# New numbers in a list scheduler's model, a fixed order for the first weight loads, and 15 matmuls of the identity while TensorE waits for them

## The chip, the cores and the metric

The kernel runs on one core of one Trainium2 chip. The metric is the device time of one execution in microseconds (us), the median of several runs. The core has a tensor engine (PE in the profile, its weight loads PEld), a vector engine (DVE), a scalar engine (ACT), GpSimd (POOL), and a queue on SyncE (SP) that issues the DMA transfers.

## The reference, cut to what is computed

A block of a diffusion transformer, two layers deep, over 256 latent and 256 context tokens of width 1024, all in float32. For each layer:

```python
mod = silu(c) @ w_ada[l] + b_ada[l]             # shift, scale and gate, for both sublayers
h = x * (1 + sc1) + sh1
q, k, v of 4 mixers, gates = split(h @ w_in[l])
y_i = latent attention, 2-D neighbourhood attention, differential attention, grouped-query attention
acc = sum_i sigmoid(gates_i) * (y_i @ w_branch[l, i])
x = layer_norm(ALPHA * x + g1 * (acc @ w_out[l]))
h = x * (1 + sc2) + sh2
x = layer_norm(ALPHA * x + g2 * ((silu(h @ Wg) * (h @ Wu)) @ w_down[l]))
```

The context tokens go through the same first layer; in the second only their keys and values are needed. The output is the latent stream.

## The kernel before

**Precision.** Every large product is made of three matmuls: an operand is split into a rounded high part and the rest (`hh`, `hl` for activations, `wh`, `wl` for weights, `fh`, `fl` for the rows of `w_out`), and `mm3` adds high by high, high by low and low by high in PSUM. For each weight tile of 128x1024 that SP loads into a `wr` buffer, ACT casts the high part (`wh` or `fh`) and DVE subtracts (`wl` or `fl`); then the `wr` buffer can take the next load. PE works mostly on moving tiles of 512 or 256 columns.

**Who decides the order.** No instruction is placed by hand. The body of the kernel only records operations in a `Plan`; `forward` then makes a list schedule of all of them. For every operation it has a modelled duration (`price`), for DMA transfers a model of one shared queue, and among the operations that are ready on an engine it takes the one with the best priority. The priorities come from `backward`, which schedules the same operations from the end. Ten passes alternate, and the one with the shortest modelled length is emitted. So a number in `price` has no direct effect on the chip: it changes which operation stands ahead of which on PE, ACT, DVE and SP. On the chip every engine goes through its list in that order, and an operation that waits holds up everything behind it on its engine. All recorded instructions have L540, the line that emits them; the strips, below, are written out at L538.

**The start.** `first_h` makes the first layer's shift and scale in eight chunks q, while weights stream in. For a chunk SP loads two tiles of `w_ada0`; the function `strips` multiplies each with the conditioning vector `cc` in float32 (four matmuls of 32x256 beside one another, into `st`; the profile counts them as eight). ACT copies `st` to `y`, PE transposes it with the identity `ident` (two transposes), DVE adds up `ada` and makes `G`, ACT makes the modulated `raw` from `x`, `ada` and `G`, and DVE casts `hh` and subtracts `hl`. `early(q)` loads the part of the input weights `w_a0` that this chunk needs and splits it; the matmuls `o<-hh,wh`, `mm<-hh,wh` and so on then use chunk q's `hh` and `hl`.

**The rest of a layer.** The input projection, the four mixers with their heads, the branch projections and `w_out`, then the feed-forward part. The shift and scale vectors of later places are made by DVE in passes over 128x1024 tiles of `w_ada` (`y<-wr,silbc` and `raw<-wr,silbc`), spread among the other work.

Of the kernel before, what the change touches and what calls it, by code (L numbers as in the profile page):

```python
# [11 lines left out]
F32R = mybir.dt.float32r  # L12
# [192 lines left out]
class Op:  # L205
    __slots__ = ("eng", "meth", "args", "kw", "phase", "idx", "preds", "succs", "npred", "tiles", "cost",
                 "prio", "prio2", "rest", "nafter", "start", "end", "est", "nrot", "bytes", "dge", "ins", "lab")

# [23 lines left out]
class Plan:  # L232
# [16 lines left out]
    def record(self, eng, meth, args, kw):  # L249
# [5 lines left out]
        if pos:  # L255
            if "out" in kw:
                ins += pos
            else:
                outs.append(pos[0])
                ins += pos[1:]  # L260
        op.preds, op.succs, op.tiles = set(), [], []
        for w, views in ((False, ins), (True, outs)):
# [15 lines left out]
        return op  # L278

    def price(self, op, ins, outs):  # L280

        eng, kw = op.eng, op.kw
        if eng == "tensor":
            if op.meth == "matmuls":
                return sum(k["rhs"].free() for k in kw["each"]) / 2400 / 4 * (1 if kw["each"][0]["rhs"].dtype == F32R else 4) + 0.1
            if op.meth == "transpose":
                n = kw["in_"].shape[0]
                return max(64, n) * 2.1 / 2400
            n = max(64, kw["rhs"].free())
            return n / 2400 + 0.0026 if kw["rhs"].dtype == F32R else n * 4 / 2400 + 0.43  # L290
        n = max([v.free() for v in outs + ins] or [1])
# [12 lines left out]
        if eng == "gpsimd":  # L304
            if kw.get("op") == ALU.pow:
                return 0.3 + n * 0.17
            return 0.16 + n * 2.2e-3
        op_bytes = 1
        for v in (outs or ins):
            op_bytes = v.shape[0] * v.free() * 4  # L310
        op.bytes = op_bytes
        op.dge = 0.65 if outs and ins else 0.46
        return 0.05
# [21 lines left out]
    def backward(self, order):  # L335
# [4 lines left out]
        for op in order:  # L340
            after = set(op.succs)
            for t in op.tiles:
                if t.next is not None:
                    after |= t.next.users
            op.nafter, op.rest = len(after), 0.0
            heirs[op] = after
# [9 lines left out]
        while done < len(order):  # L356
# [10 lines left out]
            if e == "sync":  # L367
                dma = max(dma, t + 0.95) + max(op.bytes / 360e3, op.dge)
                free[e] = dma - 0.95
                op.prio2 = dma + 1.1  # L370
            else:
                free[e] = op.prio2 = t + op.cost
            done += 1
            for p in before[op]:
                p.rest = max(p.rest, op.prio2 + SEE[p.eng].get(e, SEE_OTHER[p.eng]))
                p.nafter -= 1
                if p.nafter == 0:
                    ready[p.eng].append(p)
# [5 lines left out]
    def forward(self):  # L384
        ops = self.ops
        for op in ops:
            op.npred = len(op.preds)
            op.est = 0.0
            op.nrot = 0
            for t in op.tiles:  # L390
                t.left, t.slot, t.waiters, t.next, t.users = 0, None, [], None, set()
# [70 lines left out]
        while done < len(ops):  # L462
# [16 lines left out]
            if e == "sync":  # L479
                dge_free = max(op.end, dge_free) + op.dge  # L480
                dma_free = max(dge_free + 0.65, dma_free) + op.bytes / 360e3
                op.end = dma_free + 0.95
                free[e] = max(free[e], dma_free - 2.5)
# [4 lines left out]
            for s in op.succs:  # L488
                s.est = max(s.est, op.end + SEE[e].get(s.eng, SEE_OTHER[e]))
                s.npred -= 1  # L490
                if s.npred == 0 and s.nrot == 0:
                    push(s)
# [50 lines left out]
class Net:  # L543
# [157 lines left out]
    def first_h(self):  # L701
# [17 lines left out]
        nk = fw // P  # L719
        kp = 512 // fw  # L720
        for q in range(NQ):
            ps = self.st_bank()
            for p in range(KT // kp):
# [8 lines left out]
                n += 1  # L732
                nc.sync.dma_start(out=raw, in_=io["w_ada0"][:, q, p * 1024:(p + 1) * 1024])
                self.strips(ps, s4, raw, p * kp, p == 0, p == 1)
            if q == 0:
# [7 lines left out]
            for j in range(2):  # L743
                nc.tensor.transpose(out=pt[:, j * P:(j + 1) * P], in_=row[:, j * P:(j + 1) * P], identity=self.ident)
            a = ada[:, :, :16].rearrange("p s (m k) -> p m s k", m=2)[:, :, :, q]
# [5 lines left out]
            for i in range(nk):  # L751
                k = nk * q + i
                self.modulate([(x[:, i * T + s * NL:i * T + (s + 1) * NL], (G[:, s], ada[:, s, :KT]), k)
                               for s in (LAT, CTX)], self.hh[:, k, :], self.hl[:, k, :], self.ap, 1)
            self.early(q)

    def strips(self, ps, s4, w, k0, first, last):

        each = [dict(out=ps[32 * i:32 * i + 32, :256], lhsT=s4[:, k0 + i, :], rhs=w[:, i * 256:(i + 1) * 256],
                     start=first, stop=last) for i in range(4)]  # L760
        self.nc.tensor.matmuls(out=ps[:, :256], each=each, lhsT=s4[:, k0:k0 + 4, :], rhs=w)

    def early(self, q):
# [3 lines left out]
        raw = self.w_tile("wr", F32)[:, :EARLY * P]  # L767
        self.nc.sync.dma_start(out=raw, in_=self.io["w_a0"][:, q, :])
        if q % 2 == 0:
# [11 lines left out]
        for b0, b1, hi, lo, o, u in cuts:  # L781
            m = (b1 - b0) * P
            self.split(hi[:, o:o + m], lo[:, u:u + m], raw[:, b0 * P:b1 * P])
            for i in range(b1 - b0):
                self.ahead[b0 + i][0].append(hi[:, o + i * P:o + (i + 1) * P])
                self.ahead[b0 + i][1].append(lo[:, u + i * P:u + (i + 1) * P])

    def modulate(self, parts, hi, lo, pool, a):
# [1036 lines left out]
```

## Time and profile before

| what | value |
|---|---|
| time, median of 3 runs | 1368.88 us (1368.81 to 1370.12) |
| profiled execution, its own time | 1369.86 us |
| span of that execution, first to last instruction | 1367.9 us |
| PE busy | 1347.7 us, 99% |
| DVE busy | 989.7 us, 72% |
| ACT busy | 643.1 us, 47% |
| granted TensorE clock, mean | 0.998 of full speed |

The profiled execution took 1.96 us more than its span, and 0.98 us more than the median of the timed runs. A row of a timeline joins equal neighbours: 'x8' behind it is their number, and the second figure is the time from the first one's start to the last one's end. Matmuls overlap in PE's pipeline, so the pace of PE is read from the starts of successive rows and not from their durations.

### The profile page before, as it was taken

How to read it: one execution, taken by the hardware profiler on the slowest of the kernel's cores; microseconds unless marked ns; L12 is line 12 of the kernel's file. 1: busy time of each engine (PE TensorE's matmuls, PEld its weight loads, DVE VectorE, ACT ScalarE, POOL GpSimd, SP SyncE). 2: the span in 40 equal slices, each digit the busy share in tenths (PEclk: the TensorE clock that was granted, in tenths of full speed). 3: DMA queues.
4: the chain of work that ended last, by engine and by line, in shares of the span. 5: the costliest groups of instructions: out<-in, count | busy, mean ns of one | idle time of the engine just before them, and what ended most of it. 6: DMA issues, size and time to landing. Idle time of an engine off the chain costs nothing.

```text
span 1367.9 us, 20685 instructions
## 1 busy us (share of the span) xinstructions
PE 1347.7 (99%) x7804; PEld 1171.5 (86%) x7804; DVE 989.7 (72%) x1753; ACT 643.1 (47%) x1160; POOL 65.4 (5%) x124
## 2 busy tenths in 40 slices
PE   7999999999999999999999999999999999999997
PEld 4789889888878889888888888899999899899986
DVE  3697899997875778777655463868979878855554
ACT  3576676633754422223222121467857566544430
POOL 0000100122000000000000000101000200000000
PEclk9999999999999999999999999999999999999999
DMA  8843534355246615556666754355344367565550
GB/s 305 290 131 103 162 103 120 103 161 155 80 151 201 209 45 160 174 185 198 216 190 198 216 183 133 104 161 161 106 135 148 125 209 270 192 186 181 186 180 31
DMA packets 72819, 223.83 MB, mean 164 GB/s; under 512 B 9696, under 2 KB 13968, under 8 KB 72720
## 3 DMA queue, kind: packets, MB, share of 16 engines
q1 hardware_dynamic: 72720, 222.52, 51.1%
q8 instruction: 61, 1.00, 0.3%
q14 instruction: 38, 0.31, 0.1%
HBM read 212.76 MB, written 1.07 MB: 156 GB/s over the span
## 4 chain that ended last, share of the span: by engine, by line
PE 92%; DVE 2%; DMA 2%; ACT 1%; POOL 1%; issue 1%; SPq 0%; POOLq 0%; DVEq 0%; ACTq 0%
PE mm L540 81%; PE st L540 7%; PE o L540 3%; DMA wr<-in_w_out 1%; PE st L538 1%; DVE wl L540 1%; DMA wr<-in_w_ada 1%; ACT wh L540 0%; DMA wr<-in_w_ckv 0%; POOL rms L540 0%; DVE x L540 0%; POOL rk L540 0%; DMA wr<-in_w_br 0%; DMA q<-raw 0%; DVE raw L540 0%
## 5 line engine op out<-in xcount | busy, mean ns | idle before, releaser
L540 ACT CAST wh<-wr 128x1024 fp32r<-128x1024 f32 (+2 forms) x261 | 265.8, 1024 | 388.4 <-PE mm L540 310.8
L540 PE MATMUL mm<-hh,wh 128*128 128x512 f32 (+1 forms) x1248 | 424.0, 341 | 1.4 <-ACT wh L540 1.0
L540 PE MATMUL mm<-hl,wh 128*128 128x512 f32 (+1 forms) x1246 | 423.1, 340 | 0.0
L540 PE MATMUL mm<-hh,wl 128*128 128x512 f32 (+1 forms) x1248 | 422.7, 340 | 0.0
L540 DVE TENSOR_TENSOR wl<-wr,wh 128x1024 fp32r<-128x1024 f32 (+3 forms) x260 | 308.9, 1192 | 151.5 <-ACT wh L540 147.7
L540 PEld LDWEIGHTS mm<-hh,wh 128*128 128x128 f32 x1248 | 235.9, 189 | 27.5 <-ACT wh L540 2.0
L540 PEld LDWEIGHTS mm<-hh,wl 128*128 128x128 f32 x1248 | 235.5, 189 | 24.6 <-issue 0.4
L540 PEld LDWEIGHTS mm<-hl,wh 128*128 128x128 f32 x1246 | 236.0, 189 | 23.4 <-DVE hl L540 0.3
L540 DVE CUSTOM_DVE_ANT_0 y<-wr,silbc 128x1024 bf16<-128x1024 f32 x80 | 96.6, 1223 | 42.4 <-DMA wr<-in_w_ada 42.4
L540 PE MATMUL mm<-wl,hh 128*128 128x256 f32 (+3 forms) x344 | 110.5, 322 | 0.0
L540 PE MATMUL mm<-wh,hh 128*128 128x256 f32 (+3 forms) x344 | 110.4, 323 | 0.0
L540 PE MATMUL mm<-wh,hl 128*128 128x256 f32 (+3 forms) x344 | 110.2, 321 | 0.0
L540 PE MATMUL mm<-wl,fh 128*128 128x512 f32 (+1 forms) x270 | 102.1, 378 | 0.0
L540 PE MATMUL mm<-wh,fh 128*128 128x512 f32 (+1 forms) x270 | 101.3, 376 | 0.0
L540 PE MATMUL mm<-wh,fl 128*128 128x512 f32 (+1 forms) x270 | 101.1, 375 | 0.0
L540 DVE TENSOR_REDUCE s<-st 128x1 f32<-128x512 f32 (+1 forms) x120 | 70.7, 598 | 8.7 <-PE st L540 6.8
L540 ACT ACTIVATE P<-st,s 128x512 f32<-128x512 f32 (+1 forms) x96 | 59.1, 617 | 28.7 <-DVE s L540 27.7
L540 PEld LDWEIGHTS mm<-wh,hh 128*128 128x128 f32 x344 | 64.8, 189 | 4.9 <-DVE y L540 0.5
L540 PE MATMUL mm<-y,wh 128*128 128x512 f32 (+1 forms) x256 | 68.7, 344 | 0.2 <-ACT wh L540 0.2
L540 PEld LDWEIGHTS mm<-wh,hl 128*128 128x128 f32 x344 | 65.0, 189 | 3.9
L540 PEld LDWEIGHTS mm<-wl,hh 128*128 128x128 f32 x344 | 65.0, 189 | 3.8
L540 DVE TENSOR_TENSOR ptl<-st,pth 128x512 fp32r<-128x512 f32 (+1 forms) x96 | 56.7, 596 | 8.0 <-ACT pth L540 7.1
(267 smaller groups left out, 1956.4 us busy)
## 6 DMA issues: line engine op xcount, KB each, us to landing
wr<-in_w_ada SPq DMA_DIRECT2D x87, 512.0 KB, 3.7
wr<-in_w_gu SPq DMA_DIRECT2D x80, 512.0 KB, 4.4
wr<-in_wa SPq DMA_DIRECT2D x74, 512.0 KB, 3.9
wr<-in_w_dn SPq DMA_DIRECT2D x44, 512.0 KB, 3.3
wr<-in_w_br SPq DMA_DIRECT2D x16, 512.0 KB, 3.5
wr<-in_w_out SPq DMA_DIRECT2D x16, 512.0 KB, 5.1
wr<-in_w_gq SPq DMA_DIRECT2D x8, 512.0 KB, 3.4
bc<-in_lnrows SPq DMA_DIRECT2D x16, 256.0 KB, 3.3
```

Source lines behind the costliest of these rows:

```text
L538: o.ins = nc.tensor.matmul(**{k: real(v) for k, v in m.items()})
L540: o.ins = getattr(getattr(nc, o.eng), o.meth)(*args, **kw)
```

## The change

It has three parts.

**The model's numbers.** In `price` a float32 strip matmul loses its factor of four, a matmul has a floor of 256 columns and a fixed part of 0.013 to 0.016 us, a transpose costs 0.108 us instead of 0.112, and GpSimd's operations get other sizes. The model of the DMA queue moves 340 instead of 360 KB per us, and what it brings is held to land later by `late`: 1.5 us for copies on the chip (`q<-raw`, `k<-k`, `row<-bcr`), 0.4 us for loads.

**An order without data.** `follow(first, then)` makes `then` come behind `first` in the schedule, with no data between them. The two `w_ada0` loads of chunks 1 to 3 are put behind the `w_a0` load of the chunk before.

**The identity by itself.** `awake(m)` records m float32 matmuls of `ident` by `ident`, 128x128, into an `o` bank that nobody reads: 8 at the very start, 2 behind each of the two strip groups of chunk 0, 3 behind its transposes, 15 in all.

```diff
+    def follow(self, first, then):
+        then.order.append(first)
+        first.heels.append(then)
...
-                return sum(k["rhs"].free() for k in kw["each"]) / 2400 / 4 * (1 if kw["each"][0]["rhs"].dtype == F32R else 4) + 0.1
+                return sum(k["rhs"].free() for k in kw["each"]) / 2400 + 0.1
             if op.meth == "transpose":
-                n = kw["in_"].shape[0]
-                return max(64, n) * 2.1 / 2400
-            n = max(64, kw["rhs"].free())
-            return n / 2400 + 0.0026 if kw["rhs"].dtype == F32R else n * 4 / 2400 + 0.43
+                return 0.108 if kw["in_"].shape[0] > 32 else 0.09
+            n = max(256, kw["rhs"].free())
+            return n / 2400 + (0.0134 if n < 512 else 0.0156)
...
-        op.dge = 0.65 if outs and ins else 0.46
+        op.dge, op.late = (0.65, 1.5) if outs and ins else (0.46, 0.4)
...
-                dma = max(dma, t + 0.95) + max(op.bytes / 360e3, op.dge)
-                free[e] = dma - 0.95
+                dma = max(dma, t + 0.95 + op.late) + max(op.bytes / 340e3, op.dge)
+                free[e] = dma - 0.95 - op.late
...
+        def awake(m, behind=None):
+            d = self.bank(self.po, "o")
+            for _ in range(m):
+                op = nc.tensor.matmul(out=d[:, :P], lhsT=self.ident, rhs=self.ident, start=True, stop=True)
+                if behind is not None:
+                    nc.follow(behind, op)
+        awake(8)
+        behind = None
...
-                nc.sync.dma_start(out=raw, in_=io["w_ada0"][:, q, p * 1024:(p + 1) * 1024])
-                self.strips(ps, s4, raw, p * kp, p == 0, p == 1)
+                ld = nc.sync.dma_start(out=raw, in_=io["w_ada0"][:, q, p * 1024:(p + 1) * 1024])
+                if behind is not None:
+                    nc.follow(behind, ld)
+                op = self.strips(ps, s4, raw, p * kp, p == 0, p == 1)
+                if q == 0:
+                    awake((2, 2)[p], op)
...
+            if q == 0:
+                awake(3, op)
...
-            self.early(q)
+            ld = self.early(q)
+            behind = ld if q < 3 else None
```

The 15 matmuls apart, the instructions are the same in number and size; only their order differs, in hundreds of places on PE, DVE and ACT, in some 120 on SP and in none on POOL. L540 and L538 become L549 and L547.

PE's list at the start of the program, before. `st` is the bank of the strips and transposes, `wr` and `l` are the two tiles of `w_ada0`, `mm` and `o` are accumulation banks.

```order
L538 MATMUL st_187<-wr_71,cc_0_97 32x256 x4
L538 MATMUL st_187<-l_0_234,cc_0_97 32x256 x4
L540 MATMUL st_188<-ident_60,y_0_87 128x128 x2
L538 MATMUL st_189<-wr_73,cc_0_97 32x256 x4
L540 MATMUL o_193<-hh_83,wh_74 128x512
L540 MATMUL mm_180<-hh_83,wh_74 128x512
L540 MATMUL mm_181<-hh_83,wh_74 128x512
L538 MATMUL st_189<-l_1_235,cc_0_97 32x256 x4
L540 MATMUL o_193<-hl_84,wh_74 128x512
L540 MATMUL o_193<-hh_83,wl_77 128x512
L540 MATMUL mm_180<-hl_84,wh_74 128x512
L540 MATMUL mm_180<-hh_83,wl_77 128x512
```

And after the change:

```order
L549 MATMUL o_193<-ident_60 128x128 x8
L547 MATMUL st_187<-wr_71,cc_0_97 32x256 x4
L549 MATMUL o_270<-ident_60 128x128 x2
L547 MATMUL st_187<-l_0_234,cc_0_97 32x256 x4
L549 MATMUL o_279<-ident_60 128x128 x2
L549 MATMUL st_188<-ident_60,y_0_87 128x128 x2
L549 MATMUL o_286<-ident_60 128x128 x3
L547 MATMUL st_189<-wr_73,cc_0_97 32x256 x4
L549 MATMUL o_306<-hh_83,wh_74 128x512
L549 MATMUL mm_180<-hh_83,wh_74 128x512
L549 MATMUL mm_181<-hh_83,wh_74 128x512
L547 MATMUL st_189<-l_1_235,cc_0_97 32x256 x4
```

The matmuls of the identity stand ahead of the first strips, behind each of them and behind the transposes; what follows on chunk 0's `hh` has kept its order.

PE's list in the first layer's input projection, at about 149 us of the trace, before. The four `raw` tiles, which ACT and POOL finish, are transposed through `ident` into `mm`.

```order
L540 MATMUL mm_1738<-hh_83,wl_1650 128x512
L540 MATMUL mm_1738<-hh_83,wh_1639 128x512
L540 MATMUL mm_1782<-ident_60,raw_1694 128x128
L540 MATMUL mm_1782<-ident_60,raw_1711 128x128
L540 MATMUL mm_1782<-ident_60,raw_1746 128x128
L540 MATMUL mm_1782<-ident_60,raw_1754 128x128
L540 MATMUL mm_1738<-hl_84,wh_1639 128x512
```

And after the change:

```order
L549 MATMUL mm_1739<-hh_83,wh_1646 128x512
L549 MATMUL mm_1739<-hl_84,wh_1646 128x512
L549 MATMUL mm_1739<-hh_83,wl_1656 128x512
L549 MATMUL mm_1739<-hh_83,wh_1646 128x512
L549 MATMUL mm_1739<-hl_84,wh_1646 128x512
L549 MATMUL mm_1793<-ident_60,raw_1707 128x128
L549 MATMUL mm_1793<-ident_60,raw_1744 128x128
L549 MATMUL mm_1793<-ident_60,raw_1758 128x128
L549 MATMUL mm_1793<-ident_60,raw_1765 128x128
L549 MATMUL mm_1739<-hh_83,wl_1656 128x512
```

Four more matmuls on `hh` and `hl` now stand ahead of these four transposes; behind them one such matmul instead of three comes before the next four.

ACT's list in the first layer's branch projections and `w_out`, at about 422 to 431 us, before. `fh` is the high part of a `w_out` tile, `wh` of a branch or gate tile.

```order
L540 CAST wh_4874<-wr_4839 128x1024
L540 ACTIVATE y_0_4882<-mm_4835 128x512
L540 CAST fh_4699<-wr_4893 128x1024
L540 CAST wh_4919<-wr_4853 128x1024
L540 CAST wh_4926<-wr_4869 128x1024
L540 ACTIVATE y_3_4939<-mm_4886 128x512
L540 CAST fh_4699<-wr_4946 128x1024
L540 CAST wh_4976<-wr_4934 128x1024
```

And after the change:

```order
L549 CAST wh_4893<-wr_4849 128x1024
L549 ACTIVATE y_0_4900<-mm_4856 128x512
L549 CAST wh_4931<-wr_4878 128x1024
L549 ACTIVATE y_1_4939<-mm_4902 128x512
L549 CAST wh_4947<-wr_4885 128x1024
L549 CAST fh_4718<-wr_4955 128x1024
L549 CAST wh_4989<-wr_4912 128x1024
L549 ACTIVATE y_0_4998<-mm_4949 128x512
L549 CAST fh_4718<-wr_4994 128x1024
```

The cast of a `w_out` tile that stood ahead of two `wh` casts has moved behind both; the load of that tile has moved in the same way on SP, behind three loads of gate tiles (`in_wa`) instead of two.

At about 1084 us, in the second layer, the two matmuls `st<-k,q` that open a head's scores stood behind five matmuls on one `wh` tile. They now stand behind 13 of them, and six of eight transposes of `qr`, from which the loads `q<-raw` follow, have moved up by six matmuls.

Between DVE's 12th and 24th head result (`y<-o,ot`, 195.11 and 281.05 us in the trace) DVE had 4 passes over `w_ada` tiles and 10 `wl` subtractions of 128x1024; it now has 8 and 13. In the same stretch PE had 248 matmuls of 512 columns and has 272.

## Rows read from the trace of the kernel before

**Rows 1.** The page, head and part 1: span, busy us, share, instructions.
```profile
span 1367.9 us, 20685 instructions
...
PE 1347.7 (99%) x7804; PEld 1171.5 (86%) x7804; DVE 989.7 (72%) x1753; ACT 643.1 (47%) x1160; POOL 65.4 (5%) x124
```

**Rows 2.** Waits of PE from 16 us on: total us, times, longest us.
```profile
PE mm L540 <- DVE wl L540: 1.4, 1, 1.4
PE mm L540 <- ACT wh L540: 1.2, 3, 0.5
PE mm L540 <- ACT raw L540: 0.6, 1, 0.6
PE st L540 <- DMA q<-raw: 0.5, 1, 0.5
```

**Rows 3.** Timeline of PE, 0 to 18 us: start, us, engine, line, operation, count.
```profile
4.96 1.08 PE L538 MATMUL st<-wr,cc 128*32 128x256 f32 x8 [4.96 <-DMA wr<-in_w_ada]
...
8.01 0.69 PE L540 MATMUL st<-ident,y 128*128 128x128 f32 x2 [0.49 <-ACT y L540]
...
10.41 1.08 PE L538 MATMUL st<-wr,cc 128*32 128x256 f32 x8 [1.72 <-DMA wr<-in_w_ada]
...
11.43 0.80 PE L540 MATMUL o<-hh,wh 128*128 128x512 f32 x1
...
13.01 1.08 PE L538 MATMUL st<-l,cc 128*32 128x256 f32 x8
...
15.71 0.38 PE L540 MATMUL st<-ident,y 128*128 128x128 f32 x2
...
17.64 0.64 PE L538 MATMUL st<-silbc,cc 128*32 128x256 f32 x8
```

**Rows 4.** Timelines of POOL, ACT and DVE, 0 to 16 us.
```profile
1.00 0.29 POOL masks.py:199 TENSOR_SCALAR_AFFINE_SELECT ident<-ident 128x128 f32<-128x128 f32 x1
...
9.03 0.83 ACT L540 CAST wh<-wr 128x768 fp32r<-128x768 f32 x1 [1.08 <-DMA wr<-in_w_a]
...
9.77 1.09 ACT L540 ACTIVATE raw<-x,ada,G 128x256 f32<-128x256 f32 x2
...
10.89 0.43 DVE L540 CAST hh<-raw 128x512 fp32r<-128x512 f32 x1
```

**Rows 5.** Timeline of PE, 149 to 151 us.
```profile
149.20 0.39 PE L540 MATMUL mm<-hh,wh 128*128 128x512 f32 x1
149.43 0.49 PE L540 MATMUL mm<-ident,raw 128*128 128x128 f32 x3
150.56 0.33 PE L540 MATMUL mm<-ident,raw 128*128 128x128 f32 x1 [0.64 <-ACT raw L540]
```

**Rows 6.** Timelines of ACT and PE, 424 to 432 us.
```profile
428.30 1.05 ACT L540 CAST fh<-wr 128x1024 fp32r<-128x1024 f32 x1 [5.02 <-DMA wr<-in_w_out]
...
429.26 2.00 ACT L540 CAST wh<-wr 128x1024 fp32r<-128x1024 f32 x2
...
429.43 0.39 PE L540 MATMUL mm<-y,wh 128*128 128x512 f32 x1
...
430.35 0.50 PE L540 MATMUL mm<-hh,wh 128*128 128x512 f32 x1 [0.53 <-ACT wh L540]
```

**Rows 7.** Timeline of PE, 1082 to 1086 us.
```profile
1083.46 0.28 PE L540 MATMUL mm<-hl,wh 128*128 128x256 f32 x1
1084.21 0.70 PE L540 MATMUL st<-k,q 128*128 128x512 f32 x2 [0.47 <-DMA q<-raw]
```

**Rows 8.** Busy us by window and engine; a DVE group of the first window.
```profile
195.11:281.05 85.94, 85.94 (x503) 74.72 (x503) 81.16 (x194) 57.73 (x144) 6.87 (x14) 1.00 0.40 121
...
200.00:220.00 20.00, 20.00 (x109) 16.93 (x108) 18.38 (x48) 11.20 (x27) 0.00 (x0) 1.00 0.44 119
...
220.00:240.00 20.00, 20.00 (x148) 18.91 (x147) 19.41 (x48) 16.10 (x42) 0.00 (x0) 1.00 0.46 133
...
L540 DVE TENSOR_TENSOR wl<-wr,wh 128x1024 fp32r<-128x1024 f32 x10 | 12.1, 1214 | 0.0
```

More of the change, by code (lines that the diff above doesn't have):

```diff
@@ L206 @@
     __slots__ = ("eng", "meth", "args", "kw", "phase", "idx", "preds", "succs", "npred", "tiles", "cost",
-                 "prio", "prio2", "rest", "nafter", "start", "end", "est", "nrot", "bytes", "dge", "ins", "lab")
+                 "prio", "prio2", "rest", "nafter", "start", "end", "est", "nrot", "bytes", "dge", "late", "ins", "lab", "order", "heels")
 class _Eng:
@@ L260, in record @@
                 ins += pos[1:]
-        op.preds, op.succs, op.tiles = set(), [], []
+        op.preds, op.succs, op.tiles, op.order, op.heels = set(), [], [], [], []
         for w, views in ((False, ins), (True, outs)):
@@ L305, in price @@
             if kw.get("op") == ALU.pow:
-                return 0.3 + n * 0.17
-            return 0.16 + n * 2.2e-3
+                return 0.4 + n * 0.17
+            return 0.3 + n * 0.6e-3
         op_bytes = 1
@@ L340, in backward @@
         for op in order:
-            after = set(op.succs)
+            after = set(op.succs) | set(op.heels)
             for t in op.tiles:
@@ L374, in backward @@
             for p in before[op]:
-                p.rest = max(p.rest, op.prio2 + SEE[p.eng].get(e, SEE_OTHER[p.eng]))
+                if op not in p.heels:
+                    p.rest = max(p.rest, op.prio2 + SEE[p.eng].get(e, SEE_OTHER[p.eng]))
                 p.nafter -= 1
@@ L386, in forward @@
         for op in ops:
-            op.npred = len(op.preds)
+            op.npred = len(op.preds) + len(op.order)
             op.est = 0.0
@@ L480, in forward @@
                 dge_free = max(op.end, dge_free) + op.dge
-                dma_free = max(dge_free + 0.65, dma_free) + op.bytes / 360e3
-                op.end = dma_free + 0.95
+                dma_free = max(dge_free + 0.65, dma_free) + op.bytes / 340e3
+                op.end = dma_free + 0.95 + op.late
                 free[e] = max(free[e], dma_free - 2.5)
@@ L489, in forward @@
                 s.est = max(s.est, op.end + SEE[e].get(s.eng, SEE_OTHER[e]))
+                s.npred -= 1
+                if s.npred == 0 and s.nrot == 0:
+                    push(s)
+            for s in op.heels:
                 s.npred -= 1
@@ L743, in first_h @@
             for j in range(2):
-                nc.tensor.transpose(out=pt[:, j * P:(j + 1) * P], in_=row[:, j * P:(j + 1) * P], identity=self.ident)
+                op = nc.tensor.transpose(out=pt[:, j * P:(j + 1) * P], in_=row[:, j * P:(j + 1) * P],
+                                         identity=self.ident)
+            if q == 0:
+                awake(3, op)
             a = ada[:, :, :16].rearrange("p s (m k) -> p m s k", m=2)[:, :, :, q]
@@ L760, in strips @@
                      start=first, stop=last) for i in range(4)]
-        self.nc.tensor.matmuls(out=ps[:, :256], each=each, lhsT=s4[:, k0:k0 + 4, :], rhs=w)
+        return self.nc.tensor.matmuls(out=ps[:, :256], each=each, lhsT=s4[:, k0:k0 + 4, :], rhs=w)
     def early(self, q):
@@ L767, in early @@
         raw = self.w_tile("wr", F32)[:, :EARLY * P]
-        self.nc.sync.dma_start(out=raw, in_=self.io["w_a0"][:, q, :])
+        ld = self.nc.sync.dma_start(out=raw, in_=self.io["w_a0"][:, q, :])
         if q % 2 == 0:
@@ L786, in early @@
                 self.ahead[b0 + i][1].append(lo[:, u + i * P:u + (i + 1) * P])
+        return ld
     def modulate(self, parts, hi, lo, pool, a):
```

## Prediction

> **What bounds the kernel now.** I read the page's first part, then the waits of TensorE, then the timelines of the places that the waits point to. PE is busy for 1347.7 of 1367.9 us, 99% [rows 1], so no other engine can give time away: the end moves only if PE waits less or runs faster. The reader is to see that about 20 us of the span are without PE. Some 8 us of it are the layer norm at the end, which the change does not touch. From 16 us on the waits add up to little: 1.4 us once for a `wl`, 1.2 us in three waits for a `wh`, 0.6 for a `raw`, 0.5 for a `q<-raw`, and three more of 0.2 each, 4.3 us in all [rows 2]. The rest is the start: 4.96 us until the first weights land, and 1.72 us ahead of the second chunk's strips [rows 3].
>
> The start has a second loss, which no wait shows. A strip group takes 1.08 us at 4.96, 10.41 and 13.01 us and 0.64 us at 17.64, and two transposes take 0.69 us at 8.01 and 0.38 us at 15.71 [rows 3]. [...]
>
> **The price of the awake matmuls.** The trace has no matmul of `ident` by itself. The nearest rows are the strips: four matmuls side by side hold PE for 1.02 us (10.41 to 11.43) over 256 columns in float32 [rows 3]. Over 128 columns I take half, an estimate of 0.43 to 0.51 us at the low level. Eight take 3.4 to 4.1 us. They can start when `ident` is made, at 1.29 us [rows 4], and end between 4.7 and 5.4 us, where the first strips started at 4.96. At worst the strips are 0.45 us late, and the two matmuls behind each strip group add up to 1 us in a stretch that has gaps of its own. Queued behind them are the transposes, then `ada`, `G` and `raw`. What covers this is ACT: it casts `wh` from 9.03 us, and `raw` comes behind that cast at 9.77 [rows 4], while the transposes start 1.8 us earlier. The last three awake matmuls lie in the idle 1.72 us ahead of 10.41. So I cost the 15 at nothing; with that cover gone they cost up to 0.4 us.
>
> **Term 1, the clock at the start.** [...] The matmul `o<-hh,wh` still waits for `hh`, which DVE ends at 11.32 [rows 4], so it stays at 11.43. From there to the transposes at 15.71 PE needed 4.28 us for one strip group and seven matmuls of 512 columns [rows 3]. At the full clock a matmul of 512 follows the last one after 0.23 us (149.20 to 149.43) [rows 5] and a strip group holds PE for about 0.6: 7 x 0.23 + 0.6 = 2.2 us. The lead is 2.1 us, of which I take 2.0. The bounds: 2.6 us, half of the 5.3 us from 10.41 to 15.71, if `hh` came earlier too; nothing, if the clock does not rise earlier; and 0.4 us lost as above. The lead must then be kept. Loads are the danger, but from 16 us on no load of weights ends a wait of PE [rows 2], and buffers also come free earlier by the same lead.
>
> [...]
>
> **Term 2, waits that the new order removes.** At 150.56 us a transpose of `raw` waited 0.64 us for ACT [rows 5]. Four matmuls of 512 now stand ahead of the group, 4 x 0.23 = 0.92 us, more than the wait. It is gone: 0.64.
>
> At 430.35 us a matmul waited for its `wh`: it started 0.92 us after the one before, where 0.23 is the pace, so 0.69 lost. The reason stands on ACT: the cast of a `w_out` tile waited 5.02 us for its load until 428.30, and the `wh` that was needed stood behind it and started at 429.26 [rows 6]. That cast now stands behind both `wh`, and its load a place later on SP. What is late next is `fl` of that `w_out` tile, which PE does not ask for at this point: 0.69.
>
> At 1084.21 us the scores waited for `q<-raw`: 0.75 us after the matmul before, where 0.12 is the pace of 256 columns (half of 0.23) [rows 7], so 0.63. They now stand eight matmuls later, 0.96 us, and the transposes that feed `q` earlier: 0.63.
>
> Together 1.96 us. The longest wait, 1.4 us for `wl` [rows 2], is at a phase boundary where DVE and PE keep their order, so it stays. Of the rest, 0.9 us, I count nothing.
>
> **Term 3, waits that it adds.** Hundreds of places on PE, DVE and ACT have moved, and only a run shows the waits. The bounds are nothing, and about as much as was taken away, 2 us, since an order made in the same way had that much. I take the middle, 1.0 us.
>
> **Sum.** -2.0 - 1.96 + 1.0 = -3.0 us. The profiled execution took 1369.86 us, so 1366.9; the median of the timed runs lies 0.98 us lower at 1368.88, so **1365.9 us**.
>
> **Rivals.** *The clock does not rise earlier.* The awake matmuls come in four pieces, and between the last piece and 10.41 PE is still idle for part of the 1.72 us; the strips of the trace's start also were work, and did not raise it by 10.41. [...] Without Term 1 the sum is -1.0: 1367.9, within the noise.
>
> *As many new waits as removed ones.* Term 3 at its upper bound: -2.0, so 1366.9, also no measurable change. For it speaks that the numbers of the model shift everything by little, against it that the three waits that went were places where a model that brings loads too early would put them.
>
> *Fewer waits than I count.* Term 1 at 2.6, the other 0.9 us of waits gone too and nothing added: 1369.86 - 2.6 - 1.96 - 0.9 = 1364.4, as a median 1363.4.
>
> *VectorE becomes the bound between 195 and 281 us, and the kernel slower.* DVE was busy for 81.16 of 85.94 us there [rows 8]. It now has seven more passes over 128x1024 between the same two head results, at 1.214 us each [rows 8], 8.5 us, so 89.7. PE has 24 more matmuls of 512, 5.5 us, so 91.4. DVE must be busy for 98%. The 20 us from 200 on reached 92% (18.38 of 20) and those from 220 on 97% (19.41) [rows 8], with no wait of PE in either. If DVE gets no further than 92%, the stretch takes 89.7 / 0.92 = 97.5 us, 6.1 more than PE's 91.4: 1365.9 + 6.1 = 1372.0, slower. At 97% it loses 1.1 us; from about 94% down it takes back the whole gain, and below 92.5% it shows as slower. Against it: DVE comes to the 12th head with less work behind it than before, since some of its passes were moved from ahead of that point, so the surplus is partly a shift of the two marks.
>
> **How the numbers follow.** A change of 0.2%, 2.7 us, is about what a measurement can tell from none, so faster means under 1366.1. Chances: my forecast 0.45, reaching from 1364.2 to 1367.0 and lying below 1366.1 in about 0.36; clock not raised 0.18 (same); waits replaced 0.15 (same, in 0.03 just faster); fewer waits 0.12 (faster); VectorE bound 0.10 (0.06 slower, 0.04 same). Faster 0.51, same 0.43, slower 0.06. The range reaches from 1362.8, below the best case by what its small terms leave open, to 1368.6, which holds the case without the clock and leaves out most of the VectorE case.
>
> **What would show it right or wrong.** Term 1: in the timeline of PE the strips near 10.4 us take 0.64 and not 1.08 us, and the chunk's transposes come at about 13.7 us instead of 15.7. Price: the first eight awake matmuls end near 4.9 us, and `raw` stays at 9.8. Term 2: no waits for ACT `raw`, for `wh` near 430, for `q<-raw`. Term 3: the sum of PE's waits from 16 us on is about 3.3 us. The forecast is wrong if strips at 10.4 us are slow, if a load of weights ends a wait between 16 and 60 us (the lead handed back), or if DVE ends long waits between 195 and 281 us.

## The result and the profile after

The changed kernel takes 1379.45 us (median of 4 runs, 1378.57 to 1379.81) where the kernel before took 1368.86 us on the same chip. The ratio is 1.0074, with a 95% interval of 1.0057 to 1.0092: 10.6 us slower. The profiled execution took 1379.35 us, its span 1377.6 us.

The page of the changed kernel, head and part 1:

```profile
span 1377.6 us, 20746 instructions
...
PE 1356.1 (98%) x7834; PEld 1176.1 (85%) x7834; DVE 984.7 (71%) x1753; ACT 642.3 (47%) x1160; POOL 69.6 (5%) x124
```

PE is still the bound, with 98% where it had 99% [rows 1]. No other engine has filled up: DVE and ACT have the same work as before. What grew is the time that PE loses between its matmuls. The waits of PE in the changed kernel from 16 us on, the longest groups:

```profile
PE mm L549 <- DVE qr L549: 2.1, 4, 0.9
PE mm L549 <- DVE wl L549: 1.4, 2, 1.0
PE mm L549 <- ACT raw L549: 1.0, 2, 0.8
PE o L549 <- ACT pth L549: 0.9, 1, 0.9
PE mm L549 <- DVE gt L549: 0.8, 2, 0.5
PE st L549 <- DMA q<-raw: 0.7, 1, 0.7
PE mm L549 <- ACT wh L549: 0.6, 2, 0.4
```

All groups of this view add up to 9.5 us in 21 waits; before it was 4.3 us in 9 waits [rows 2]. That is 5.2 of the 9.7 us by which the span grew. The rest lies in delays that this view does not list. They can be estimated from the starts of PE's matmuls in both traces, each distance to the next start set against the usual one for the same shapes: from 17.7 us on, places that lose 0.3 us or more grew from 9 to 21 and by about 7 us together, and some 40 more places of 0.03 to 0.3 us cost about 3 us.

Where it happened can be read from a landmark that both programs have, the transpose of the finished `ada` vector. The timeline of PE in the kernel before, late in the first layer's mixers, behind its gate and up matmuls, and late in the second layer's mixers:

```profile
402.19 0.27 PE L540 MATMUL st<-ident,ada 128*8 128x128 f32 x1
...
746.61 0.38 PE L540 MATMUL st<-ident,ada 128*8 128x128 f32 x2
...
1116.15 0.27 PE L540 MATMUL st<-ident,ada 128*8 128x128 f32 x1
```

And in the changed kernel:

```profile
406.59 0.27 PE L549 MATMUL st<-ident,ada 128*8 128x128 f32 x1
...
750.70 0.38 PE L549 MATMUL st<-ident,ada 128*8 128x128 f32 x2
...
1124.77 0.27 PE L549 MATMUL st<-ident,ada 128*8 128x128 f32 x1
```

The first stretch, with the first layer's mixers, loses 4.4 us; the second, with `w_out` and most of the feed-forward part, nothing (-0.3); the third, with the second layer's mixers, 4.5; and what follows 1.1, so that the end is 9.7 us late. So most of the loss lies in the two stretches where many short chains through DVE, ACT, GpSimd and copies feed PE, and it is spread over them.

The start looks as follows; the timeline of PE in the changed kernel:

```profile
1.34 3.58 PE L549 MATMUL o<-ident 128*128 128x128 f32 x16 [1.34 <-POOL ident masks.py:199]
5.03 0.64 PE L547 MATMUL st<-wr,cc 128*32 128x256 f32 x8
...
10.17 0.64 PE L547 MATMUL st<-wr,cc 128*32 128x256 f32 x8 [1.32 <-DMA wr<-in_w_ada]
11.32 0.69 PE L549 MATMUL o<-hh,wh 128*128 128x512 f32 x1 [0.51 <-DVE hh L549]
...
12.80 1.08 PE L547 MATMUL st<-l,cc 128*32 128x256 f32 x8
...
17.43 0.64 PE L547 MATMUL st<-silbc,cc 128*32 128x256 f32 x8
```

And its windows around the place where the pace breaks, with the granted clock behind the five engines' busy times:

```profile
10.00:11.00 1.00, 0.64 (x8) 0.16 (x8) 0.96 (x2) 0.71 (x2) 0.00 (x0) 1.00 0.98 388
...
12.00:13.00 1.00, 1.00 (x7) 0.35 (x9) 0.00 (x0) 0.00 (x0) 0.00 (x0) 0.50 1.06 431
...
15.00:16.00 1.00, 1.00 (x7) 0.80 (x6) 0.45 (x4) 0.00 (x0) 0.00 (x0) 1.00 1.05 417
```

The eight first matmuls took 3.58 us, and behind them the clock was up: the strips take 0.64 us at 5.03 and 10.17 us, where they took 1.08 [rows 3]. But PE then stood idle for 1.32 us ahead of 10.17 and for 0.51 us ahead of 11.32, and the granted clock fell to 0.50, until nearly 15 us; the strips at 12.80 us take 1.08 us again. (In this view 1.00 alone is no proof of the faster pace: the kernel before has 1.00 from 10 to 11 us too, where a strip group takes 1.08 us.) At 17.43 us PE is 0.2 us ahead of the kernel before, not 2.

### The profile page after: what moved, and what is told of

The parts are those of the page before. It is cut to its first block, busy times and chain, and to the rows that moved or that the text cites. A ratio compares the mean times of both kernels' runs of the same rounds, so it can differ in the third digit from the quotient of the medians.

```text
span 1377.6 us, 20746 instructions
## 1 busy us (share of the span) xinstructions
PE 1356.1 (98%) x7834; PEld 1176.1 (85%) x7834; DVE 984.7 (71%) x1753; ACT 642.3 (47%) x1160; POOL 69.6 (5%) x124
## 4 chain that ended last, share of the span: by engine, by line
PE 83%; DVE 9%; ACT 3%; POOL 2%; issue 2%; DMA 1%; SPq 0%; POOLq 0%; DVEq 0%; ACTq 0%
PE mm L549 74%; PE st L549 6%; PE o L549 3%; DVE s L549 2%; DVE wl L549 2%; ACT P L549 1%; POOL rms L549 1%; DVE raw L549 1%; DVE P L549 1%; DVE ptl L549 1%; ACT wh L549 1%; DVE x L549 1%; POOL rk L549 1%; PE st L547 1%; DVE y L549 0%
## 5 line engine op out<-in xcount | busy, mean ns | idle before, releaser
L549 ACT CAST wh<-wr 128x1024 fp32r<-128x1024 f32 (+2 forms) x261 | 266.1, 1024 | 395.5 <-PE mm L549 333.7
L549 PE MATMUL mm<-hh,wh 128*128 128x512 f32 (+1 forms) x1248 | 424.3, 341 | 2.0 <-DVE gt L549 0.8
L549 PE MATMUL mm<-hh,wl 128*128 128x512 f32 (+1 forms) x1248 | 423.7, 340 | 0.4 <-DVE wl L549 0.4
L549 PE MATMUL mm<-hl,wh 128*128 128x512 f32 (+1 forms) x1246 | 422.5, 339 | 0.0
L549 DVE TENSOR_TENSOR wl<-wr,wh 128x1024 fp32r<-128x1024 f32 (+3 forms) x260 | 308.7, 1191 | 143.0 <-ACT wh L549 141.3
L549 PEld LDWEIGHTS mm<-hh,wh 128*128 128x128 f32 x1248 | 235.9, 189 | 28.0 <-ACT wh L549 2.8
L549 PEld LDWEIGHTS mm<-hh,wl 128*128 128x128 f32 x1248 | 235.7, 189 | 25.0 <-DVE wl L549 0.6
L549 PEld LDWEIGHTS mm<-hl,wh 128*128 128x128 f32 x1246 | 236.0, 189 | 23.4 <-issue 0.4
L549 DVE CUSTOM_DVE_ANT_0 y<-wr,silbc 128x1024 bf16<-128x1024 f32 x80 | 96.4, 1220 | 39.4 <-DMA wr<-in_w_ada 39.4
L549 PE MATMUL mm<-wh,hh 128*128 128x256 f32 (+3 forms) x344 | 110.2, 322 | 0.3 <-DVE kz L549 0.3
L549 PE MATMUL mm<-wl,hh 128*128 128x256 f32 (+3 forms) x344 | 110.3, 321 | 0.0
L549 PE MATMUL mm<-wh,hl 128*128 128x256 f32 (+3 forms) x344 | 109.8, 321 | 0.0
L549 PE MATMUL mm<-wl,fh 128*128 128x512 f32 (+1 forms) x270 | 102.1, 378 | 0.0
L549 PE MATMUL mm<-wh,fh 128*128 128x512 f32 (+1 forms) x270 | 101.6, 376 | 0.0
L549 PE MATMUL mm<-wh,fl 128*128 128x512 f32 (+1 forms) x270 | 101.0, 375 | 0.0
L549 ACT ACTIVATE P<-st,s 128x512 f32<-128x512 f32 (+1 forms) x96 | 59.0, 616 | 33.4 <-DVE s L549 31.9
L549 DVE TENSOR_REDUCE s<-st 128x1 f32<-128x512 f32 (+1 forms) x120 | 69.9, 594 | 2.2 <-PE st L549 1.1
L549 PEld LDWEIGHTS mm<-wh,hh 128*128 128x128 f32 x344 | 64.8, 189 | 4.8 <-issue 0.4
L549 PEld LDWEIGHTS mm<-wl,hh 128*128 128x128 f32 x344 | 65.0, 189 | 4.0
L549 PEld LDWEIGHTS mm<-wh,hl 128*128 128x128 f32 x344 | 64.8, 189 | 3.7
L549 PE MATMUL mm<-y,wh 128*128 128x512 f32 (+1 forms) x256 | 66.8, 341 | 0.2 <-ACT wh L549 0.2
L549 DVE CUSTOM_DVE_ANT_0 raw<-wr,silbc 128x1024 bf16<-128x1024 f32 x48 | 58.0, 1215 | 3.3 <-DMA wr<-in_w_ada 3.2
```

The source lines that it names most:

```text
L549: o.ins = getattr(getattr(nc, o.eng), o.meth)(*args, **kw)
```

## The experiments

The three parts of the change separate cleanly, because the order of each program can be read: without its 15 matmuls of the identity the changed kernel keeps every other row, and `follow` alone moves no row at all, as the old order already had these loads where it puts them. Theories on trial: **A**, the new numbers give a worse order, the matmuls of the identity are nearly free; **B**, the start is to blame. Under A: **A1**, the order loses slack because PE is no longer too fast in the model; **A2**, the DMA numbers; **G**, GpSimd's numbers; **A3**, any shift costs, as the order of before was a lucky one.

**e1_numbers_alone**, the change without the matmuls of the identity:

```diff
-        awake(8)
...
-                    awake((2, 2)[p], op)
...
-                awake(3, op)
```

> The change without its 15 matmuls of the identity; on every engine the order is otherwise the change's own. Theory A (the new numbers give an order with more waits, the matmuls of the identity are nearly free): 1379 to 1381 us, and PE's waits from 16 us on add up to about 10 us as in the changed kernel. Rival B (the matmuls of the identity, and the clock that rises and falls again with them, upset the start and what follows): below 1374 us.

1380.34 us, ratio 1.0079 (1.0063 to 1.0096). The whole loss is there without them. B falls.

**e2_awake_alone**, the kernel before with the 15 matmuls and none of the numbers.

> The kernel before with the 15 matmuls of the identity and none of the new numbers; the rest of the order is that of before but for a few rows at the start. Theory A: 1368.0 to 1369.0 us, since the clock falls back behind them and gives only some tenths. Rival B: 1373 us or more.

1369.52 us, ratio 1.0001 (0.9991 to 1.0010): nothing gained, nothing lost. As the old numbers price each of them at 0.64 us, a few rows of the start have moved; in its timeline PE idles for 1.53 us ahead of the transposes at 10.14 us, and the strips at 10.73 and 11.58 us take 1.08 us again. The mean granted clock of its ten runs is 0.996 or 0.997.

**e3_price_alone** and **e4_dma_alone**, the two halves of the numbers:

```diff
+            n = max(256, kw["rhs"].free())
+            return n / 2400 + (0.0134 if n < 512 else 0.0156)
```

```diff
+        op.dge, op.late = (0.65, 1.5) if outs and ins else (0.46, 0.4)
```

> The kernel before with the new durations of matmuls, transposes and GpSimd in the model, and the old DMA numbers. Theory A1 (PE was too fast in the old model, which made the schedule put the other engines' work early; with the true pace that slack is gone): 1375 us or more. Rival A2 (the DMA numbers, which move loads and copies on SP, do the harm): 1371 us or less. Rival A3 (any shift of the numbers gives an order that is worse by some us, because before was the best of many): both single parts slower, by amounts that do not add up.

> The kernel before with the new DMA numbers (340 KB per us, late 1.5 and 0.4 us) and the old durations. A1: 1371 us or less. A2: 1375 us or more. A3: slower than 1371 us too, though nothing in it takes slack from the other engines.

e3: 1386.50 us, ratio 1.0125 (1.0110 to 1.0140), 17.2 us slower. e4: 1372.68 us, ratio 1.0024 (1.0014 to 1.0033), 3.4 us slower. Both together cost 11.1 (e1), less than the first alone. A2 falls as the main cause; A1 and A3 both stand, and that the parts do not add up speaks for A3.

**e5_matmul_numbers**, **e6_gpsimd_numbers**: the durations split again, into PE's and GpSimd's.

> The kernel before with the new durations of matmuls, strips and transposes alone (a matmul of 512 columns 0.229 instead of 0.216 us in the model); the numbers of GpSimd and of the DMA queue are the old ones. A1 (the schedule loses the slack that a too fast PE in the model had given the other engines): about as slow as both durations together, 1380 to 1387 us. Rival G (it is GpSimd, whose longer operations the new numbers halve, so that what waits for it comes too early): 1372 us or less. A3 (any shift of the numbers costs some us): 1371 to 1380 us.

> The kernel before with the new numbers of GpSimd alone. A1: within 2 us of before, 1367 to 1371 us. Rival G: 1378 us or more. A3: 1371 to 1380 us.

e5: 1388.37 us, ratio 1.0142 (1.0128 to 1.0156). e6: 1375.09 us, ratio 1.0040 (1.0026 to 1.0053). Neither A1 nor G forecast both; again they do not add up (19.3 and 6.1 us apart, 17.2 together).

**e7_matmul_still_faster** and **e11_tiny_shift**, controls that move one number of the kernel before a little to either side:

```diff
-            return n / 2400 + 0.0026 if kw["rhs"].dtype == F32R else n * 4 / 2400 + 0.43
+            return n / 2400 + 0.0 if kw["rhs"].dtype == F32R else n * 4 / 2400 + 0.43
```

```diff
+            return n / 2400 + 0.0030 if kw["rhs"].dtype == F32R else n * 4 / 2400 + 0.43
```

> The kernel before with the constant in a matmul's modelled duration moved the other way, from 0.0026 to 0 us: PE is 1.2% faster still in the model for 512 columns, and the other engines keep a little more slack. It moves some 2,500 of PE's rows, as many as the durations alone did. A1: no worse than before, 1366 to 1370 us. A3 (before was the best of many orders, so any new one is worse): 1372 us or more.

> The kernel before with the constant of a matmul at 0.0030 instead of 0.0026 us in the model, 0.2% of a matmul of 512 columns; it moves some 1,700 of PE's rows. A3 (before is the best of many orders, and a new one costs 3 to 20 us whichever way the numbers move): 1372 us or more. If the loss grows with the size of the shift: within 1.5 us of before.

e7: 1380.97 us, ratio 1.0080 (1.0062 to 1.0099). e11: 1375.28 us, ratio 1.0043 (1.0029 to 1.0057). This decides between A1 and A3. In e7 the other engines had more slack and it was 11.9 us slower; in e11 the number moved by 0.0004 us and it cost 6.1. Their waits are of the kinds that the changed kernel has too, in other sizes. The longest of PE's waits from 16 us on in e7:

```profile
PE st L540 <- DMA q<-raw: 2.5, 2, 2.4
PE mm L540 <- ACT raw L540: 2.5, 1, 2.5
```

Not all of e7's loss is waiting. The wait for `raw` ends at 152.36 us, and the windows behind it show a lower granted clock, here 154 to 156 us:

```profile
154.00:156.00 2.00, 2.00 (x7) 1.57 (x7) 1.38 (x2) 1.53 (x2) 0.00 (x0) 0.55 0.15 59
```

Of e7's four runs the two with a mean granted clock of 0.994 and 0.995 took 1382.45 and 1382.76 us, the two with 0.998 took 1375.78 and 1379.48. So the wait for `raw` was paid for a second time, in the slower matmuls behind it; even the fastest of the four is 6.7 us slower than before.

And in e11, where one wait of 2.4 us is the one that [rows 6] show at 430 us, grown, with the same `w_out` cast ahead:

```profile
PE mm L540 <- ACT wh L540: 3.4, 5, 2.4
```

**e8_fill_the_gaps** and **e12_fill_six** turn to the start. On the order of before the matmuls of the identity are priced at 0.2 us, and more of them bridge PE's gaps (9 behind the first transposes in e8, 6 in e12, 3 in the change) and 2 stand behind the second chunk's first strips; no other row moves but a pair of neighbours on PE.

```diff
+                awake(9, op)
...
+                if q == 1 and p == 0:
+                    awake(2, op)
```

> The kernel before with 23 matmuls of the identity: 8, 2 and 2 as in the change, 9 instead of 3 behind the first transposes and 2 more behind the second chunk's first strips, so that PE hardly idles until 11.3 us. They cost 0.2 us each in the model, and every other row keeps the order of before. [...]

> As e8_fill_the_gaps, with 6 instead of 9 matmuls of the identity behind the first transposes: in e8 nine ran until 10.9 us and held up strips whose load had come by 10.4. If the clock stays up, the second chunk's strips start at 10.3 to 10.4 us at 0.64 us, and the lead at 17 us is 1.7 us instead of 1.2. Of it some 0.5 to 1 us lasts to the end, as part of e8's lead was given back at 430 us: 1367 to 1368.3 us. If three matmuls fewer let the clock fall: as e2_awake_alone, within 0.5 us of before.

e8: 1368.28 us, ratio 0.9992 (0.9983 to 1.0001). e12: 1367.49 us, ratio 0.9988 (0.9979 to 0.9997), 1.7 us faster than before and the fastest version here. The timeline of PE in e12:

```profile
10.90 0.64 PE L550 MATMUL st<-wr,cc 128*32 128x256 f32 x8 [0.60 <-DMA wr<-in_w_ada]
...
12.90 0.64 PE L550 MATMUL st<-l,cc 128*32 128x256 f32 x8
...
16.42 0.64 PE L550 MATMUL st<-silbc,cc 128*32 128x256 f32 x8
```

The clock now stays up, and the row that stood at 17.64 us [rows 3] stands at 16.42, a lead of 1.2 us. In the 22 runs of e8 and e12 the mean granted clock is 0.998 or 0.999. My expectation for e12 had one thing wrong: the strips at 10.90 us wait for their load, not for the nine matmuls. The load landed half a microsecond later than in the other traces, and the lead shrank by that. The matmul of [rows 6] at 430.35 us comes at 429.95 us in e8, where its wait has grown to 1.15 us, so that most of e8's lead was given back there:

```profile
429.95 0.50 PE L552 MATMUL mm<-hh,wh 128*128 128x512 f32 x1 [1.15 <-ACT wh L552]
```

**e9_no_pow_after** and **e10_no_pow_before** replace GpSimd's powers by products when the program is written out, so that neither price nor order changes and the norms are left out of the computation:

```diff
+                        if o.eng == "gpsimd" and kw.get("op") == ALU.pow:
+                            kw["op"], kw["in0"] = ALU.mult, kw["in1"]
```

> The changed kernel, every row in its place, with GpSimd's power operations (the inverse roots of the norms) replaced by products of a constant, so that the norms are left out of the computation; the model still counts them as powers. If the chains through GpSimd cause the waits for DVE qr and ACT raw (3.3 us with their restarts nearer 4), these go and the time falls to 1375 to 1376.5 us. If those waits have another source behind GpSimd, or the next one in the queue takes their place: 1378 us or more.

> The kernel before with the same replacement, for the same chains in its order: they cost it 0.6 us for ACT raw and 0.2 us for DVE qr, so 1368 to 1368.5 us, 1 us at most below before. If GpSimd costs both orders alike, it falls by as much as the changed kernel does, 3 us or more.

e9: 1374.64 us, ratio 1.0037 (1.0024 to 1.0051), so 5.5 us above before instead of 10.6. e10: 1368.82 us, ratio 0.9996 (0.9987 to 1.0005). With the powers gone the changed order is 5.1 us faster, and the order of before gains nearly nothing, with the same operations in both. In e9 PE's waits for `raw` are gone and those for `qr` are down from 2.3 us to 0.5.

Not all of the 5.1 us are GpSimd's. The start of e9 has the changed kernel's rows, but in its profiled execution the clock did not fall. The timeline of PE in e9:

```profile
10.47 0.64 PE L549 MATMUL st<-wr,cc 128*32 128x256 f32 x8 [1.45 <-DMA wr<-in_w_ada]
11.62 0.47 PE L551 MATMUL o<-hh,wh 128*128 128x512 f32 x1 [0.51 <-DVE hh L551]
...
16.21 0.64 PE L549 MATMUL st<-silbc,cc 128*32 128x256 f32 x8
```

The last of these rows stood at 17.43 us in the changed kernel, so 1.2 us of the difference were there before any of GpSimd's chains, and from there to the end e9's profiled execution is 3.9 us shorter. PE idled no less here than in the changed kernel (1.45 and 0.51 us against 1.32 and 0.51), so these gaps alone do not decide whether the clock falls. The mean granted clock was 0.997 in 3 of the 4 runs of the changed kernel and in 1 of the 5 of e9, and 0.998 or 0.999 in the others.

**e13_gpsimd_probe** measures the pair of GpSimd operations by itself. 


> No mixer at all: a small kernel that only runs GpSimd's pair of operations on 128x1 (scale and add, then power), six pairs in each of five stages: alone; beside VectorE passes over 128x1024 in SBUF; beside VectorE operations of 128x32; beside VectorE reductions of 128x512 from PSUM; beside ScalarE casts of 128x1024. If VectorE's long passes stretch GpSimd's operations, a pair takes about 0.8 us alone and 1.5 us or more beside the passes. If not, and the long operations in the changed kernel have another source (the data, the semaphores), a pair takes 0.8 us in all stages.

Some groups of GpSimd in that kernel (stage `n` alone, `p` beside DVE's passes over 128x1024, `q` beside its reductions from PSUM), with busy us and the mean of one in ns:

```profile
L549 POOL TENSOR_TENSOR sp<-sp,half 128x1 f32<-128x1 f32 x6 | 6.3, 1044 | 0.5
L549 POOL TENSOR_SCALAR sp<-a 128x1 f32<-128x1 f32 x6 | 4.0, 671 | 0.4
L549 POOL TENSOR_TENSOR sn<-sn,half 128x1 f32<-128x1 f32 x6 | 3.3, 552 | 0.5
L549 POOL TENSOR_TENSOR sq<-sq,half 128x1 f32<-128x1 f32 x6 | 3.3, 552 | 0.5
...
L549 POOL TENSOR_SCALAR sn<-a 128x1 f32<-128x1 f32 x6 | 1.1, 190 | 1.2 <-DVE a L549 0.8
```

A pair takes 0.74 us alone and beside the reductions, 0.74 to 0.75 in the two stages that are not shown (beside small DVE operations and beside ACT's casts), and 1.72 us on average beside DVE's passes. The average hides that the passes ended halfway through that stage; the timelines of DVE and GpSimd there:

```profile
8.21 10.03 DVE L549 TENSOR_TENSOR wp<-a,b 128x1024 fp32r<-128x1024 f32 x8
...
15.85 1.53 POOL L549 TENSOR_TENSOR sp<-sp,half 128x1 f32<-128x1 f32 x1
17.45 0.84 POOL L549 TENSOR_SCALAR sp<-a 128x1 f32<-128x1 f32 x1
18.37 0.55 POOL L549 TENSOR_TENSOR sp<-sp,half 128x1 f32<-128x1 f32 x1
```

While they last, a power takes 1.53 us and the pair 2.4, over three times what it takes alone.

**e14_no_pow_copy_first** is e9 with one row of SP moved in the second layer: the load of a branch tile goes behind four copies instead of ahead of them.

```diff
-DMA wr<-in_w_br 128x1024
 DMA k<-k 64x512
 DMA q<-raw 64x256
 DMA k<-k 64x512
 DMA q<-raw 64x256
+DMA wr<-in_w_br 128x1024
```

> As e9_no_pow_after (the changed order, the norms left out), with one row of SP moved: in the second layer the 512 KB load of a branch tile, which is issued just ahead of the copies k<-k and q<-raw, is issued behind the first four of them. If that load is what makes the copies land late, the scores' wait of 1.8 us for q<-raw goes and the time falls by 1.5 to 2 us from e9's 1374.6. If the copies are late because they are issued late, it stays within 0.7 us.

1372.68 us, ratio 1.0032 (1.0021 to 1.0044): 3.9 us above before, where e9 was 5.5. The DMA issues around 1085 us, with the median time to landing, first in e9:

```profile
k<-k SPq DMA_DIRECT2D x2, 128.0 KB, 6.7
q<-raw SPq DMA_DIRECT2D x4, 64.0 KB, 6.7
```

and in e14:

```profile
k<-k SPq DMA_DIRECT2D x2, 128.0 KB, 2.9
q<-raw SPq DMA_DIRECT2D x4, 64.0 KB, 2.6
```

PE's wait of 1.8 us for `q<-raw` is gone, and with the load just ahead of them the copies took some 4 us longer to land. A second load, of a `wa` tile, stands ahead of the copies in both. The times alone show the gain less clearly: e14 is 1.6 us faster than e9 by the medians, but the intervals of the two ratios overlap. In the profiled executions e14 is 0.3 us ahead of e9 at the row near 16 us and 2.4 us at the end.

**e15_gpsimd_priced_slow** gives the changed kernel's model the stretched price:

```diff
-                return 0.4 + n * 0.17
-            return 0.3 + n * 0.6e-3
+                return 1.4 + n * 0.17
+            return 0.9 + n * 0.6e-3
```

> The changed kernel with GpSimd's operations priced as they take beside VectorE's passes (power 1.57 us instead of 0.57 on one column, the others 0.9 instead of 0.3), so that the schedule keeps room for the chains; the rest of the change stays. It moves some 1,700 of PE's rows against the changed kernel. If the missing room for these chains is what makes its order slow, PE's waits for DVE qr and ACT raw fall from 3.3 us to under 1 us, and the time to 1372 to 1376 us. If orders scatter whatever the model says (A3), those waits may go and others come: anywhere from 1372 to 1390 us, with the sum of PE's waits from 16 us on no smaller than the changed kernel's 11 us.

1375.53 us, ratio 1.0044 (1.0027 to 1.0061): 6.5 us above before, where the changed kernel was 10.6 above. The waits for `qr` fell from 2.3 to 0.2 us. Those for `raw` did not (1.3 us in two waits, 1.0 in the changed kernel).

The result lies in the expected band, but one order cannot tell a mended price from a luckier draw; the waits for `qr` fit the first, those for `raw` the second.

## Why the prediction was wrong

**The bound and the price of the matmuls of the identity** were right. PE has 98%, the eight took 3.58 us (3.4 to 4.1 foreseen; of the two figures for one, 0.51 us is half of a strip group, and 0.43 an estimate that no row there gives), and e2 shows them free.

**Term 1, 2.0 us: failed as to this kernel.** The step that failed is the one that put seven matmuls of 512 columns and a strip group at the pace of the full clock, 2.2 us from 11.43 us to the transposes. That the clock would be up by 10.4 us, and would stay up, was my estimate; no row of the kernel before shows it. The first half came true, with 0.64 us for the strips at 10.17 us, but in the profiled execution the clock did not stay up, and the lead at 17.43 us was 0.2 us. I had the idle time ahead of 10.4 us in the rival "the clock does not rise earlier" and priced it as no rise; in fact the clock rose and fell again. e9 and e12 show that the term itself existed: with the same start rows and the clock up, e9's lead is 1.4 us at 16.21 us; with the gaps bridged, e12's is 1.2 us and the kernel 1.7 us faster. So the order alone does not settle whether the clock falls; that bridging helps is what the mean granted clocks say (0.998 or more in all 22 runs of e8 and e12, 0.996 or 0.997 in the ten of e2). The moment of the rise varied too: behind the same eight matmuls of the identity the first strips took 0.64 us in the changed kernel, 1.06 us, at 5.11 us, in e9, which has the same order, and 1.08 us, at 5.06 us, in e2 and e8.

**Term 2, 1.96 us of removed waits: one of three.** At 430 us the reading was right: the changed kernel has no wait of PE between 412 and 450 us, and the `w_out` cast waits on ACT with nothing urgent behind it. At 149 us four more matmuls did stand ahead of the transposes, yet PE waited 0.81 us where it had waited 0.64 [rows 5], because what it waits for came later too. The timeline of GpSimd there, in the kernel before and in the changed kernel:

```profile
148.18 1.81 POOL L540 TENSOR_TENSOR rk<-rk,mhalf 128x1 f32<-128x1 f32 x2
...
147.34 1.32 POOL L549 TENSOR_SCALAR rk<-s 128x1 f32<-128x1 f32 x2
148.75 2.75 POOL L549 TENSOR_TENSOR rk<-rk,mhalf 128x1 f32<-128x1 f32 x2
```

I took the arrival of `raw` as fixed and moved only the one who waits. The two powers took 2.75 us instead of 1.81, and the last `raw` came 1.5 us later. In both traces DVE passes over 128x1024 run beside these powers, at other moments; that the passes stretched them fits e13 and is not shown by itself. At 1084 us I counted eight matmuls and the earlier transposes, but not the load that now stands ahead of the copies on SP. SP's queue in the kernel before, then SP's queue and PE's wait in the changed kernel:

```profile
1080.47 1.14 SPq L540 DMA_DIRECT2D q<-raw  x2
...
1083.63 0.53 SPq L540 DMA_DIRECT2D wr<-in_w_br  x1
...
1086.94 0.33 SPq L549 DMA_DIRECT2D wr<-in_w_br  x1
1087.32 0.50 SPq L549 DMA_DIRECT2D k<-k  x1
1087.87 1.07 SPq L549 DMA_DIRECT2D q<-raw  x1
...
1093.73 0.70 PE L549 MATMUL st<-k,q 128*128 128x512 f32 x2 [0.75 <-DMA q<-raw]
```

Before, that load was issued behind the copies, and the first `q<-raw` landed 3.6 us after its issue; now it takes 5.7 us, and the wait went from 0.47 [rows 7] to 0.75 us.

**Term 3, waits that the new order adds: the step that made the prediction wrong.** The bound "about as much as was taken away, 2 us, since an order made in the same way had that much" took the order of before for a typical one. It is not: eight sets of numbers, from 0.0004 us on one constant to the whole change, gave orders 3.4 to 19.3 us slower, and none equal. (Orders that differ from before in their first rows alone, e2, e8 and e12, cost nothing.) What a new order takes away and adds is by these runs not a gain of about 1 us, but a loss of 3 to 19. In the changed kernel itself the net loss is 9.9 us from 17 us on, where 2 us were the most that I allowed for new waits. That every set tried was slower is shown; that the numbers of before had been chosen by the time they gave would explain it, and is only argued.

**What the 10.6 us consist of.** By the medians, each against before, e9 takes away 5.1 us and e14 another 1.6, and 3.9 are left. Of the 5.1 some 1.2 go to the clock at the start in the profiled executions, so the chains through GpSimd cost about 4. The copies cost their 1.6 us only once the powers are gone: in the changed kernel PE's wait for `q<-raw` is 0.75 us, in e9 1.8. What is left is not explained by waits that the view lists: in e14 they add up to 4.8 us, before to 4.3. It lies for the most part in the short delays told of above, which no run isolated. It stays open, as does how much of e15's gain is its price.

**VectorE as the bound** was the rival on the slower side, and it did not happen in the place named. Between the same two head results, at 192.34 and 287.72 us in the changed kernel, DVE was busy for 92.23 of 95.38 us, the 97% at which the rival loses 1.1 us and not 6.1, and PE waited once, for 0.3 us:

```profile
192.34:287.72 95.38, 95.10 (x546) 81.85 (x545) 92.23 (x213) 62.55 (x154) 6.55 (x14) 1.00 0.41 122
```

If DVE had a part in the loss, it was through GpSimd.

**Two slips in the working**, which change nothing in the outcome: the listed waits that no term touches are 1.3 us (4.3 - 1.4 - 1.6), not 0.9; and VectorE would have taken back the whole gain from about 95% down (89.7 / 0.95 = 94.4, 3.0 more than 91.4), not 94%.

## What to carry to other kernels

An order that a scheduler found is a draw, and it is worth knowing how wide the draw is before pricing one: shift a constant by a hair and time it, and if that costs 6 us, a change of the model's numbers cannot be priced by the waits it removes. When a wait is to be covered by moving work ahead of it, follow the other side too, what it waits for and which engine or queue runs beside that. Where matmuls are added to raise the clock early, fill the gaps behind them too (the mean granted clock was 0.998 or 0.999 in the runs of e8 and e12, 0.996 or 0.997 in those of e2), and look at more than one execution before saying that it holds. When an operation is taken out to see what it cost, compare the traces up to the first place that it can touch: what differs there is not its doing.

## What the runs showed of the hardware

In e13 GpSimd's small operations took longer beside DVE passes over 128x1024 that read two tiles in SBUF: a power on 128x1 took 0.55 us alone and 1.53 us beside them. It kept its 0.55 us beside reductions from PSUM, beside ACT's casts and beside DVE operations of 128x32. These last also read two tiles in SBUF, so that alone does not tell which DVE operations delay GpSimd.

A granted clock that had risen fell again soon: in the changed kernel it stood at 1.00 at 10 us, with strips of 0.64 us, and at 0.50 at 12 us, with strips of 1.08 us, after PE had idled for 1.32 and 0.51 us. In e9 PE idled for 1.45 and 0.51 us at the same rows, and the pace stayed up: from the first matmul on `hh` to the strips of `silbc` it took 4.6 us (11.62 to 16.21), in the changed kernel 6.1 (11.32 to 17.43). In e7 the clock fell in the middle of the kernel, to a mean of 0.55 from 154 to 156 us, behind a wait of 2.5 us.
